# Two-layer streaming encoder on one core: table loads, ScalarE casts and GpSimd blocks are given other places in the queues around the second half's channel norm

## The chip, the cores and the metric

The program runs on one core of one Trainium2 chip. The metric is the device time of one execution in microseconds. The five queues that matter are TensorE (PE, matrix products), VectorE (DVE), ScalarE (ACT), GpSimd (POOL) and SyncE (SP, which issues the transfers). Each engine works through its own instruction queue in order.

## The reference, cut to what matters

Layer 0 mixes an S5 state-space branch and a retention branch; nothing of it is touched. Layer 1 is a Conformer convolution module, and the whole is closed by a root-mean-square norm. The input is 1 x 1024 positions x 1024 channels in float32.

```python
def mixer_conv(h, w_in, conv_w, conv_b, ln_g, ln_b, w_out):
    proj = h @ w_in
    a, b, g = jnp.split(proj, 3, axis=-1)
    u = a * jax.nn.sigmoid(b)
    u = depthwise_conv(u, conv_w, width=31, causal) + conv_b
    mu = jnp.mean(u, axis=-1, keepdims=True)
    var = jnp.mean(jnp.square(u - mu), axis=-1, keepdims=True)
    u = (u - mu) * lax.rsqrt(var + EPS) * ln_g + ln_b
    return (jax.nn.silu(u) * jax.nn.silu(g)) @ w_out

x = x + mixer_conv(rmsnorm(x, norm_g[1]), ...)
return rmsnorm(x, final_g)
```

## The kernel before, in words

Channels lie on the 128 partitions, in eight blocks numbered `nb` or `kb`. Positions lie along a row and are cut in two halves of 512, `h` = 0 and 1. Every product is made of three in a reduced format: a weight block and an operand are each split into a high and a low part (`wh`, `wl`, and for the last product `zh`, `zl`), and `mm3` issues high x high (line 181), high x low (line 182) and low x high (line 183) into one PSUM bank. The high part is a ScalarE copy that rounds (a CAST in the profile), the low part a subtraction on VectorE or GpSimd.

The last product, `w_out_c(h, nb, ...)`, is made of blocks: for each half eight output blocks `nb`, each summing over eight operand blocks `z0` to `z7`, so 24 products of 512 columns. In the text "block (h, nb)" is such an output block. A block takes its weights with `wnext`, which also starts the load of the next two weight blocks in the list: a transfer into `wf`, the ScalarE cast to `wh` (line 171, or line 148 where the low part comes back from DRAM, line 157). `wf`, `wh` and `wl` have three buffers each. When its products are done VectorE adds the residual (line 1649, `x` in the profile), ScalarE squares the sum (line 1650, `s2q`), GpSimd adds the squares up over the blocks (line 1654), and ScalarE multiplies by the final gain (line 1655).

The operand of half 1 becomes ready late. `conv_norm_wide` takes the channel norm of half 1: the last square of the convolution's output (`csquare`, line 1524), two products with a matrix of ones that sum over channels (`wide_sums`, line 487, tile `cst`), then the square of the mean (line 1595), the scaled mean `dl` (line 1598), the variance (line 1599), and in `wide_rsqrt` the factor 1/sqrt as exp(-0.5 ln v) with one Newton step: table load (line 495), Ln (line 497), Exp (line 498), Square (line 499, kept as `self.halved`), two VectorE steps (lines 500 and 501). `conv_scale` then makes the eight operands: scale by the factor (line 1611), subtract (line 1615), SiLU on ScalarE (line 1616), multiply by the gate `gl` (line 1622), split into `zh` and `zl` (lines 1232 and 1234). In half 1 GpSimd does blocks 3, 5 and 7 of these, from a copy `RL` of the factor that ScalarE makes (line 1614), and VectorE does 0, 1, 2, 4 and 6. VectorE's blocks work in a PSUM tile tagged `cv`, of which there are two, so block 2 starts when block 0 has been split, and so on.

A planner orders each engine's queue before the program runs: it simulates the program and takes, for an engine that is free, the ready instruction with the smallest priority number. `self.at(n)` sets that number: the channel norm of half 1 and its operands have 160000, the blocks of half 0 and the first blocks' stage 400000, the blocks (1, 0) to (1, 2) and the final norm of half 0 410000. `issue_after(ins)` adds an edge that holds what is traced under it behind `ins`, but only those instructions that go to the same engine as `ins`; it is an order in that engine's queue and no wait. Blocks (0, 4) to (0, 7) are held for the time in which the norm of half 1 is worked out, so that TensorE has products meanwhile:

```python
blocks(0, range(N0, N0 + 1))
with self.tc.issue_after(self.last_square.ins):
    blocks(0, range(N0 + 1, 8), {N0 + 1: {HOLD: self.norm_mm}, N0 + 2: {0: self.norm_mm}})
```

`N0` is 4, and `last_square` is the ScalarE square of the convolution's block 7. The table of SiLU is named nowhere: the compiler puts a load ahead of the first activation that needs another table (it carries line 1616). After block (1, 2) follow the final norm of half 0 (its sum over channels is tile `rf_R`) and the blocks (1, 3) to (1, 7).

Of the kernel before, what the change touches and what calls it, by code (L numbers as in the profile page):

```python
# [11 lines left out]
F32 = mybir.dt.float32  # L12
F32R = mybir.dt.float32r
I32 = mybir.dt.int32
AF = mybir.ActivationFunctionType
# [37 lines left out]
class Trunk:  # L53
# [432 lines left out]

        self.last_stat = self.nc.tensor.matmul(ps, self.ones[:], a, start=True, stop=True)

    def wide_rsqrt(self, ps, pool, name, scale=1.0):


        nc, v = self.nc, self.nc.vector
        y, half = (pool.tile([P, HALF], F32, name=f"{name}_{tag}", tag=tag, bufs=1) for tag in ("dg", "sq"))
        with self.tc.issue_after(self.squared.ins):
            table = nc.scalar.preload_act_table_set("natural_log_exp_and_others")
        with self.tc.issue_after(table.ins):
            nc.scalar.activation(y[:], ps, AF.Ln, scale=scale, bias=self.epst[:])
        nc.scalar.activation(y[:], y[:], AF.Exp, scale=-0.5)
        self.halved = nc.scalar.activation(half[:], y[:], AF.Square, scale=(0.5 * scale) ** 0.5)
        v.scalar_tensor_tensor(ps, ps, EPS / scale, half[:], op0=ALU.add, op1=ALU.mult)  # L500
        v.scalar_tensor_tensor(ps, ps, 1.5, y[:], op0=ALU.subtract, op1=ALU.mult, reverse0=True)

    def wide_rstd(self, a, pool, name):

# [726 lines left out]
    def split(self, src, hi, lo, eng, behind=None):  # L1231
        self.nc.scalar.copy(hi[:], src)  # L1232
        with self.tc.issue_after(behind.ins) if behind else nullcontext():
            eng.tensor_tensor(lo[:], src, hi[:].bitcast(F32), op=ALU.subtract)

    def layer0_back_and_layer1(self, st):
        nc, A = self.nc, self.A
# [283 lines left out]
        def csquare(h, nb, bank=None):  # L1521
            sq = bank or (self.opA.tile([P, HALF], F32, name=f"cvq{nb}_{h}", tag="A1") if h else
                  lp.tile([P, HALF], F32, name=f"cvq{nb}_{h}", tag="sq", bufs=1))
            self.squared = nc.scalar.activation(sq[:], cv[h][nb][:], AF.Square)
            return sq
# [52 lines left out]
        def conv_norm_wide(sm, acc):  # L1578


            u, w, part, co = self.last_tap
            total = ps_cv.tile([P, HALF], F32, name="cvs_bank", tag="cv")
            v.tensor_tensor(total[:], part[:], sm[:], op=ALU.add)
            v.scalar_tensor_tensor(co[:], u, w, part[:], op0=ALU.mult, op1=ALU.add)
            v.scalar_tensor_tensor(sm[:], u, w, total[:], op0=ALU.mult, op1=ALU.add)
            q7 = csquare(1, 7, ps_cv.tile([P, HALF], F32, name="cvq_bank", tag="cv"))
            self.last_square = self.squared
            self.squares_added = v.tensor_tensor(acc[:], acc[:], q7[:], op=ALU.add)
            s1, s2 = (ps_cv.tile([P, HALF], F32, name=f"cst{i}_1", tag="cn") for i in range(2))
            self.wide_sums(s1[:], sm[:])  # L1590
            self.wide_sums(s2[:], acc[:])
            self.norm_mm = self.last_stat

            m2 = lp.tile([P, HALF], F32, name="cm2_1", tag="dg", bufs=1)
            self.squared = nc.scalar.activation(m2[:], s1[:], AF.Square, scale=1.0 / D)
            dl = lp.tile([P, HALF], F32, name="dl_1", tag="cs", bufs=1)
            with self.tc.issue_after(self.squared.ins):
                nc.scalar.mul(dl[:], s1[:], 1.0 / D)
            v.scalar_tensor_tensor(s2[:], s2[:], 1.0 / D, m2[:], op0=ALU.mult, op1=ALU.subtract)
            self.wide_rsqrt(s2[:], lp, "cn_1")  # L1600
            v.tensor_tensor(dl[:], dl[:], s2[:], op=ALU.mult)
            conv_scale(1, s2, dl)

        def conv_scale(h, Rp, dl):
            R = None
            for nb in range(8):
                c = cv[h][nb]

                e1, e = (v, gp) if h == 0 else (gp, gp) if nb in (3, 5, 7) else (v, v)
                z = ps_cv.tile([P, HALF], F32, name=f"zz{nb}_{h}", tag="cv") if e is v else c  # L1610
                e1.tensor_tensor(z[:], c[:], (R if e1 is gp else Rp)[:], op=ALU.mult)
                if h and nb == 0:
                    R = lp.tile([P, HALF], F32, name=f"RL_{h}", tag="cq", bufs=1)
                    nc.scalar.copy(R[:], Rp[:])
                e.tensor_tensor(z[:], z[:], dl[:], op=ALU.subtract)
                nc.scalar.activation(z[:], z[:], AF.Silu, scale=self.vec(V_LNG, nb), bias=self.vec(V_LNB, nb))
                tag, bufs = ("ld", 2) if h == 0 else ("tp", 3) if nb < 3 else ("u", 5)
                g = lp.tile([P, HALF], F32, name=f"gl{nb}_{h}", tag=tag, bufs=bufs)

                with self.tc.issue_after(self.low_load["ca1"].ins) if h == 0 and nb < 2 else nullcontext():  # L1620
                    nc.sync.dma_start(g[:], self.gs_d[rows(nb), hs(h)])
                e.tensor_tensor(z[:], g[:], z[:], op=ALU.mult)
                pt = (self.opA, "A1") if h and nb == 7 else (opB, f"B{1 - h}")
                a, b = (self.op_tile(*pt, f"z{q}{nb}_{h}") for q in "hl")
                self.split(z[:], a, b, e)
                zs[h][nb] = (a, b)

        final = [[], []]
# [2 lines left out]
        def w_out_c(h, nb, cols, hold=None):  # L1631
# [11 lines left out]
            def part(c):  # L1643
                ps = self.bank(f"mm_oc{nb}_{h}_{c.start}", aux=False)
                n = c.stop - c.start
                self.gemm(ps[:, :n], w, [(a[:, c], b[:, c]) for a, b in zs[h]], hold)
                behind = self.behind.pop(nb, None)
                with self.tc.issue_after(behind.ins) if behind else nullcontext():
                    self.last_add = v.tensor_tensor(t[:, c], ps[:, :n], xt[:, c], op=ALU.add)
                self.squared = nc.scalar.activation(sq[:, c], t[:, c], AF.Square)  # L1650

                if 0 < nb < KB - (h == 1 and c.start > 0):
                    a = final[h][0][1]
                    gp.tensor_tensor(a[:, c], a[:, c], sq[:, c], op=ALU.add)
                nc.scalar.mul(t[:, c], t[:, c], self.vec(V_FG, nb))
            for c in cols:
                yield part(c)

# [48 lines left out]
        for h in range(2):  # L1707
# [20 lines left out]
            with self.at(400000):  # L1728
                if h == 0:
                    blocks(0, range(N0))  # L1730
                    continue

                self.behind = {N0: self.squares_added}
                blocks(0, range(N0, N0 + 1))

                with self.tc.issue_after(self.last_square.ins):
                    blocks(0, range(N0 + 1, 8), {N0 + 1: {HOLD: self.norm_mm}, N0 + 2: {0: self.norm_mm}})
            with self.at(410000):
                blocks(1, range(3))
                with self.tc.issue_after(self.last_mm.ins):  # L1740
# [123 lines left out]
```

## Time and profile before

| what | value |
|---|---|
| time, median of 3 runs (lowest, highest) | 1183.95 us (1183.84, 1184.95) |
| the profiled execution's own time | 1182.88 us |
| its span, first to last instruction | 1181.1 us |
| TensorE busy | 1169.7 us, 99% |
| VectorE, ScalarE, GpSimd busy | 848.4, 490.0, 654.7 us |
| mean granted TensorE clock | 0.999 |

A busy time counts an engine's instructions, not its use; idle time of an engine that does not set the end costs nothing. The timeline of an engine gives start, duration, engine, line, operation, tiles written and read, and in brackets the idle time before the instruction and what ended it. Products overlap, so the distance between two starts is what one product costs.

### The profile page before, as it was taken

To read this page: it belongs to the slowest core of one execution; us is meant where nothing else is said; L and a number is where in the kernel's file an instruction comes from. 1 tells how busy PE (TensorE), PEld (TensorE's weight loads), DVE (VectorE), ACT (ScalarE), POOL (GpSimd) and SP (SyncE) were. 2 spreads that over 40 slices of the span, in tenths; PEclk is the share of its full clock that TensorE was granted. 3 is DMA by queue.
4 is the path that set the end of the run, shared out by engine and by line. 5 is a ranking of instruction groups with operands and counts; after the bars stand their busy time and mean duration, and the time that the engine had idled before them with its cause. 6 is when DMAs were issued, how large, how long until landed. Compare 5 with 4: busy or idle time off the path is not lost.

```text
span 1181.1 us, 17216 instructions
## 1 busy us (share of the span) xinstructions
PE 1169.7 (99%) x6286; PEld 979.1 (83%) x6286; DVE 848.4 (72%) x1464; ACT 490.0 (41%) x719; POOL 654.7 (55%) x448
## 2 busy tenths in 40 slices
PE   9999999999999999999999999999999999999997
PEld 8788888888888888999888888888888888888776
DVE  7975697777418359486679323599999899999744
ACT  6322232322223231333446324445526675444663
POOL 2059999888136354232673111588535567667743
PEclk9999999999999999999999999999999999999999
DMA  9344345655378666769998977656678564367854
GB/s 356 102 135 137 126 150 168 191 179 174 117 266 286 234 220 213 253 221 335 377 340 295 332 261 248 227 183 214 213 251 284 209 191 162 111 200 248 279 189 177
DMA packets 117637, 261.46 MB, mean 221 GB/s; under 512 B 10672, under 2 KB 42288, under 8 KB 116912
## 3 DMA queue, kind: packets, MB, share of 16 engines
q1 hardware_dynamic: 117552, 260.36, 64.9%
q8 instruction: 49, 0.80, 0.3%
q14 instruction: 36, 0.29, 0.1%
HBM read 181.48 MB, written 74.65 MB: 217 GB/s over the span
## 4 chain that ended last, share of the span: by engine, by line
PE 96%; ACT 1%; DVE 1%; DMA 1%; issue 1%; POOL 0%; POOLq 0%; ACTq 0%
PE mm_g L181 8%; PE mm_g L183 7%; PE mm_g L182 7%; PE mm_wo L181 5%; PE mm_wo L182 5%; PE mm_wo L183 5%; PE mm_b L183 2%; PE mm_b L181 2%; PE mm_a L181 2%; PE mm_a L183 2%; PE mm_a L182 2%; PE mm_b L182 2%; PE mm_u L181 2%; PE mm_u L183 2%; PE mm_u L182 2%; PE mm_glu L181 2%
## 5 line engine op out<-in xcount | busy, mean ns | idle before, releaser
L1505 DVE SCALAR_TENSOR_TENSOR cv<-u,convw,cv 128x512 f32<-128x512 f32 x398 | 273.3, 752 | 10.0 <-ACT cv L1484 8.1
L1478 POOL TENSOR_TENSOR tp<-tp,tp 128x512 f32<-128x512 f32 x64 | 83.8, 1309 | 36.7 <-ACT tp L1477 35.6
L181 PE MATMUL mm_g<-xh,wh_g 128*128 128x512 f32 x256 | 101.8, 398 | 0.0
L183 PE MATMUL mm_g<-xh,wl_g 128*128 128x512 f32 x256 | 100.1, 391 | 0.0
L182 PE MATMUL mm_g<-xl,wh_g 128*128 128x512 f32 x256 | 100.0, 391 | 0.0
L415 POOL TENSOR_TENSOR s1q<-s1q,s1q 128x512 f32<-128x512 f32 x12 | 17.7, 1478 | 85.3 <-ACT s1q L410 85.3
L1477 ACT ACTIVATE tp<-u,convw 128x512 f32<-128x512 f32 x64 | 45.3, 719 | 33.6 <-POOL tp L1478 33.5
L181 PEld LDWEIGHTS mm_g<-xh,wh_g 128*128 128x128 f32 x256 | 48.0, 188 | 11.7 <-issue 1.2
L183 PEld LDWEIGHTS mm_g<-xh,wl_g 128*128 128x128 f32 x256 | 48.0, 188 | 10.3
L182 PEld LDWEIGHTS mm_g<-xl,wh_g 128*128 128x128 f32 x256 | 48.1, 188 | 9.9 <-issue 0.4
L371 DVE TENSOR_TENSOR gt<-mm_g,R 128x512 f32<-128x512 f32 x32 | 21.9, 684 | 46.8 <-PE mm_g L183 46.8
L181 PE MATMUL mm_oc<-zh,wh_woc 128*128 128x512 f32 (+1 forms) x144 | 53.0, 375 | 2.3 <-ACT zh L1232 2.3
L182 PE MATMUL mm_oc<-zl,wh_woc 128*128 128x512 f32 (+1 forms) x144 | 52.6, 366 | 0.0
L183 PE MATMUL mm_oc<-zh,wl_woc 128*128 128x512 f32 (+1 forms) x144 | 52.4, 366 | 0.0
L172 POOL TENSOR_TENSOR wl_glu<-wf_glu,wh_glu 128x1024 fp32r<-128x1024 f32 x14 | 34.0, 2428 | 32.9 <-ACT wh_glu L171 20.2
L172 POOL TENSOR_TENSOR wl_v<-wf_v,wh_v 128x1024 fp32r<-128x1024 f32 x12 | 31.2, 2603 | 35.0 <-ACT wh_v L171 35.0
L181 PE MATMUL mm_wo<-ysh,wh_wos 128*128 128x512 f32 x128 | 50.2, 392 | 0.0
L181 PE MATMUL mm_g<-h1h,wh_cg 128*128 128x512 f32 x128 | 50.2, 392 | 0.0
L183 PE MATMUL mm_b<-h1h,wl_cb 128*128 128x512 f32 x128 | 49.9, 390 | 0.0
L182 PE MATMUL mm_b<-h1l,wh_cb 128*128 128x512 f32 x128 | 49.8, 389 | 0.0
L182 PE MATMUL mm_wo<-ysl,wh_wos 128*128 128x512 f32 x128 | 49.8, 389 | 0.0
L183 PE MATMUL mm_g<-h1h,wl_cg 128*128 128x512 f32 x128 | 49.8, 389 | 0.0
(525 smaller groups left out, 3654.6 us busy)
## 6 DMA issues: line engine op xcount, KB each, us to landing
wf_g<-w_ab SPq DMA_DIRECT2D x16, 512.0 KB
wf_wos<-w_out SPq DMA_DIRECT2D x16, 512.0 KB
wf_wor<-w_out SPq DMA_DIRECT2D x16, 512.0 KB
wf_cb<-w_c SPq DMA_DIRECT2D x16, 512.0 KB
wf_ca<-w_c SPq DMA_DIRECT2D x16, 512.0 KB
wf_woc<-w_out_c SPq DMA_DIRECT2D x16, 512.0 KB
wf_v<-w_v SPq DMA_DIRECT2D x12, 512.0 KB
wf_cg<-w_c SPq DMA_DIRECT2D x11, 512.0 KB
```

Of the source, the lines that this page charges most:

```text
L172: self.low_made = lo[i].tensor_tensor(wl[:].rearrange(fl)[:, c], wf[:, c], h.bitcast(F32), op=ALU.subtract)
L181: nc.tensor.matmul(ps, wh[:, kb, :], xh, start=start, stop=False, **more)
L182: nc.tensor.matmul(ps, wh[:, kb, :], xl, start=False, stop=False, **more)
L183: self.last_mm = nc.tensor.matmul(ps, wl[:, kb, :], xh, start=False, stop=stop, **more)
L371: nc.vector.tensor_tensor(gt[:, c], ps[:], self.R[:, c], op=ALU.mult)
L415: nc.gpsimd.tensor_tensor(a, a, sq[:], op=ALU.add)
L1477: nc.scalar.mul(sk[:], u[:, k:k + HALF], cw[:, nb, k:k + 1])
L1478: gp.tensor_tensor(s0[:], s0[:], sk[:], op=ALU.add)
L1505: v.scalar_tensor_tensor(dst[:], *tap, accs_[i][:], op0=ALU.mult, op1=ALU.add)
```

## The change

Five things are done, all around the norm of half 1.

- `log_table`, the load of the table for Ln and Exp, is a function of its own. `conv_norm_wide` calls it first, behind the square of convolution block 6, and the square of block 7 is held behind it. For the other two callers of `wide_rsqrt` nothing changes.
- After `wide_rsqrt` a load of the SiLU table is placed behind `self.halved`, the Square of line 499.
- On ScalarE the squares of blocks (0, 4) to (0, 7) are held behind `halved`, and each final-gain product behind the square of its block. What block (0, 6) issues on ScalarE is held behind `halved`, what block (0, 7) issues there behind the first SiLU of the operands; block (0, 5) stays behind `last_square`.
- On GpSimd the steps of operand block 5 are held behind steps of block 3, and those of block 7 behind steps of block 5, by the table in `behind`.
- GpSimd's sums of squares of blocks (0, 5) to (0, 7) are held behind the low part of operand block 3.

```diff
@@ -486,19 +486,22 @@
 
         self.last_stat = self.nc.tensor.matmul(ps, self.ones[:], a, start=True, stop=True)
 
-    def wide_rsqrt(self, ps, pool, name, scale=1.0):
+    def wide_rsqrt(self, ps, pool, name, scale=1.0, table=None):
 
 
         nc, v = self.nc, self.nc.vector
         y, half = (pool.tile([P, HALF], F32, name=f"{name}_{tag}", tag=tag, bufs=1) for tag in ("dg", "sq"))
-        with self.tc.issue_after(self.squared.ins):
-            table = nc.scalar.preload_act_table_set("natural_log_exp_and_others")
+        table = table or self.log_table()
         with self.tc.issue_after(table.ins):
             nc.scalar.activation(y[:], ps, AF.Ln, scale=scale, bias=self.epst[:])
         nc.scalar.activation(y[:], y[:], AF.Exp, scale=-0.5)
         self.halved = nc.scalar.activation(half[:], y[:], AF.Square, scale=(0.5 * scale) ** 0.5)
         v.scalar_tensor_tensor(ps, ps, EPS / scale, half[:], op0=ALU.add, op1=ALU.mult)
         v.scalar_tensor_tensor(ps, ps, 1.5, y[:], op0=ALU.subtract, op1=ALU.mult, reverse0=True)
+
+    def log_table(self):
+        with self.tc.issue_after(self.squared.ins):
+            return self.nc.scalar.preload_act_table_set("natural_log_exp_and_others")
 
     def wide_rstd(self, a, pool, name):
 
@@ -1231,7 +1234,7 @@
     def split(self, src, hi, lo, eng, behind=None):
         self.nc.scalar.copy(hi[:], src)
         with self.tc.issue_after(behind.ins) if behind else nullcontext():
-            eng.tensor_tensor(lo[:], src, hi[:].bitcast(F32), op=ALU.subtract)
+            return eng.tensor_tensor(lo[:], src, hi[:].bitcast(F32), op=ALU.subtract)
 
     def layer0_back_and_layer1(self, st):
         nc, A = self.nc, self.A
@@ -1578,12 +1581,15 @@
         def conv_norm_wide(sm, acc):
 
 
+
+            table = self.log_table()
             u, w, part, co = self.last_tap
             total = ps_cv.tile([P, HALF], F32, name="cvs_bank", tag="cv")
             v.tensor_tensor(total[:], part[:], sm[:], op=ALU.add)
             v.scalar_tensor_tensor(co[:], u, w, part[:], op0=ALU.mult, op1=ALU.add)
             v.scalar_tensor_tensor(sm[:], u, w, total[:], op0=ALU.mult, op1=ALU.add)
-            q7 = csquare(1, 7, ps_cv.tile([P, HALF], F32, name="cvq_bank", tag="cv"))
+            with self.tc.issue_after(table.ins):
+                q7 = csquare(1, 7, ps_cv.tile([P, HALF], F32, name="cvq_bank", tag="cv"))
             self.last_square = self.squared
             self.squares_added = v.tensor_tensor(acc[:], acc[:], q7[:], op=ALU.add)
             s1, s2 = (ps_cv.tile([P, HALF], F32, name=f"cst{i}_1", tag="cn") for i in range(2))
@@ -1597,32 +1603,47 @@
             with self.tc.issue_after(self.squared.ins):
                 nc.scalar.mul(dl[:], s1[:], 1.0 / D)
             v.scalar_tensor_tensor(s2[:], s2[:], 1.0 / D, m2[:], op0=ALU.mult, op1=ALU.subtract)
-            self.wide_rsqrt(s2[:], lp, "cn_1")
+            self.wide_rsqrt(s2[:], lp, "cn_1", table=table)
+            with self.tc.issue_after(self.halved.ins):
+                nc.scalar.preload_act_table_set("silu_and_others")
             v.tensor_tensor(dl[:], dl[:], s2[:], op=ALU.mult)
             conv_scale(1, s2, dl)
 
         def conv_scale(h, Rp, dl):
-            R = None
+            R, steps = None, {}
+
+            def behind(nb, step, of):
+
+                ins = steps.get((nb - 2, of)) if h and nb in (5, 7) else None
+                return self.tc.issue_after(ins.ins) if ins else nullcontext()
+
             for nb in range(8):
                 c = cv[h][nb]
 
                 e1, e = (v, gp) if h == 0 else (gp, gp) if nb in (3, 5, 7) else (v, v)
                 z = ps_cv.tile([P, HALF], F32, name=f"zz{nb}_{h}", tag="cv") if e is v else c
-                e1.tensor_tensor(z[:], c[:], (R if e1 is gp else Rp)[:], op=ALU.mult)
+                with behind(nb, "scale", "sub" if nb == 5 else "low"):
+                    e1.tensor_tensor(z[:], c[:], (R if e1 is gp else Rp)[:], op=ALU.mult)
                 if h and nb == 0:
                     R = lp.tile([P, HALF], F32, name=f"RL_{h}", tag="cq", bufs=1)
                     nc.scalar.copy(R[:], Rp[:])
-                e.tensor_tensor(z[:], z[:], dl[:], op=ALU.subtract)
-                nc.scalar.activation(z[:], z[:], AF.Silu, scale=self.vec(V_LNG, nb), bias=self.vec(V_LNB, nb))
+                with behind(nb, "sub", "gate"):
+                    steps[nb, "sub"] = e.tensor_tensor(z[:], z[:], dl[:], op=ALU.subtract)
+                silu = nc.scalar.activation(z[:], z[:], AF.Silu, scale=self.vec(V_LNG, nb), bias=self.vec(V_LNB, nb))
+                if nb == 0:
+                    self.first_silu = silu
                 tag, bufs = ("ld", 2) if h == 0 else ("tp", 3) if nb < 3 else ("u", 5)
                 g = lp.tile([P, HALF], F32, name=f"gl{nb}_{h}", tag=tag, bufs=bufs)
 
                 with self.tc.issue_after(self.low_load["ca1"].ins) if h == 0 and nb < 2 else nullcontext():
                     nc.sync.dma_start(g[:], self.gs_d[rows(nb), hs(h)])
-                e.tensor_tensor(z[:], g[:], z[:], op=ALU.mult)
+                with behind(nb, "gate", "low" if nb == 7 else "gate"):
+                    steps[nb, "gate"] = e.tensor_tensor(z[:], g[:], z[:], op=ALU.mult)
                 pt = (self.opA, "A1") if h and nb == 7 else (opB, f"B{1 - h}")
                 a, b = (self.op_tile(*pt, f"z{q}{nb}_{h}") for q in "hl")
-                self.split(z[:], a, b, e)
+                steps[nb, "low"] = self.split(z[:], a, b, e)
+                if nb == 3:
+                    self.third_low = steps[nb, "low"]
                 zs[h][nb] = (a, b)
 
         final = [[], []]
@@ -1647,12 +1668,16 @@
                 behind = self.behind.pop(nb, None)
                 with self.tc.issue_after(behind.ins) if behind else nullcontext():
                     self.last_add = v.tensor_tensor(t[:, c], ps[:, :n], xt[:, c], op=ALU.add)
-                self.squared = nc.scalar.activation(sq[:, c], t[:, c], AF.Square)
+
+                with self.tc.issue_after(self.halved.ins) if h == 0 and nb >= N0 else nullcontext():
+                    self.squared = nc.scalar.activation(sq[:, c], t[:, c], AF.Square)
 
                 if 0 < nb < KB - (h == 1 and c.start > 0):
                     a = final[h][0][1]
-                    gp.tensor_tensor(a[:, c], a[:, c], sq[:, c], op=ALU.add)
-                nc.scalar.mul(t[:, c], t[:, c], self.vec(V_FG, nb))
+                    with self.tc.issue_after(self.third_low.ins) if h == 0 and nb > 4 else nullcontext():
+                        gp.tensor_tensor(a[:, c], a[:, c], sq[:, c], op=ALU.add)
+                with self.tc.issue_after(self.squared.ins):
+                    nc.scalar.mul(t[:, c], t[:, c], self.vec(V_FG, nb))
             for c in cols:
                 yield part(c)
 
@@ -1734,7 +1759,11 @@
                 blocks(0, range(N0, N0 + 1))
 
                 with self.tc.issue_after(self.last_square.ins):
-                    blocks(0, range(N0 + 1, 8), {N0 + 1: {HOLD: self.norm_mm}, N0 + 2: {0: self.norm_mm}})
+                    blocks(0, range(N0 + 1, N0 + 2), {N0 + 1: {HOLD: self.norm_mm}})
+                with self.tc.issue_after(self.halved.ins):
+                    blocks(0, range(N0 + 2, N0 + 3), {N0 + 2: {0: self.norm_mm}})
+                with self.tc.issue_after(self.first_silu.ins):
+                    blocks(0, range(N0 + 3, 8))
             with self.at(410000):
                 blocks(1, range(3))
                 with self.tc.issue_after(self.last_mm.ins):
```

## The prediction

> **What bounds the kernel now.** I read the page first, then TensorE's waits, then the queues of the engines around the longest of them.
>
> ```profile
> span 1181.1 us, 17216 instructions
> PE 1169.7 (99%) x6286; PEld 979.1 (83%) x6286; DVE 848.4 (72%) x1464; ACT 490.0 (41%) x719; POOL 654.7 (55%) x448
> PE 96%; ACT 1%; DVE 1%; DMA 1%; issue 1%; POOL 0%; POOLq 0%; ACTq 0%
> ```
>
> TensorE is busy for 99% of the span and 96% of the chain that ended last is its own. The change removes no product, so it can only win TensorE's holes. Its waits (time in total, times, longest) and its queue around the longest say where they are:
>
> ```profile
> PE mm_oc L181 <- ACT zh L1232: 2.3, 1, 2.3
> PE cst L487 <- DVE cq L1588: 0.4, 1, 0.4
> ```
>
> ```profile
> 1120.91 0.39 PE L183 MATMUL mm_oc<-zh,wl_woc 128*128 128x512 f32 x1
> ...
> 1125.65 0.39 PE L183 MATMUL mm_oc<-zh,wl_woc 128*128 128x512 f32 x1
> 1128.34 0.96 PE L181 MATMUL mm_oc<-zh,wh_woc 128*128 128x512 f32 x3 [2.30 <-ACT zh L1232]
> ...
> 1129.64 0.39 PE L181 MATMUL mm_oc<-zh,wh_woc 128*128 128x512 f32 x1
> ...
> 1140.52 0.40 PE L183 MATMUL mm_oc<-zh,wl_woc 128*128 128x512 f32 x1
> 1140.76 1.02 PE L487 MATMUL rf_R<-s2q,ones 128*128 128x512 f32 x2
> ```
>
> The row at 1120.91 is the last product of block (0, 7); from there to the row `rf_R` TensorE has the 72 products of blocks (1, 0) to (1, 2). The three first products in one row at 1128.34 show that the blocks go side by side, operand by operand. Between 1129.64 (the 24th) and 1140.52 (the 72nd) lie 48 steps without a hole: 10.88 / 48 = 0.2267 us each. Unhindered, the 72 would begin at 1120.91 + 0.23 = 1121.14 and end at 1121.14 + 72 x 0.2267 = 1137.46. `rf_R` starts at 1140.76. So **3.30 us** are lost here: 2.46 in the wait for z2's high part (1128.34 less 1125.65 + 0.23), the rest in small gaps around z0's and z2's arrival. That is the most this change can win at that place. The 0.4 us before `cst` comes before anything that it moves, and stays.
>
> Why z2 is late, on ScalarE, VectorE and GpSimd:
>
> ```profile
> 1096.20 0.63 ACT L1524 ACTIVATE cvq<-co 128x512 f32<-128x512 f32 x1 [2.46 <-DVE co L1505]
> 1098.66 1.05 ACT L171 CAST wh_woc<-wf_woc 128x1024 fp32r<-128x1024 f32 x1 [1.82 <-PE mm_oc L182]
> 1103.01 0.60 ACT L1524 ACTIVATE cvq_bank<-co 128x512 f32<-128x512 f32 x1 [3.30 <-DVE co L1584]
> ...
> 1105.57 0.59 ACT L1598 ACTIVATE dl<-cst 128x512 f32<-128x512 f32 x1
> 1106.17 1.28 ACT L495 ACT_TABLE_LOAD   x1
> 1107.47 0.72 ACT L1655 ACTIVATE x<-x,vecs 128x512 f32<-128x512 f32 x1
> 1108.10 0.61 ACT L1650 ACTIVATE s2q<-x 128x512 f32<-128x512 f32 x1
> 1108.62 0.67 ACT L497 ACTIVATE cn_dg<-cst,epst 128x512 f32<-128x512 f32 x1
> 1109.19 0.71 ACT L1655 ACTIVATE x<-x,vecs 128x512 f32<-128x512 f32 x1
> 1109.81 0.62 ACT L498 ACTIVATE cn_dg<-cn_dg 128x512 f32<-128x512 f32 x1
> 1110.33 1.03 ACT L148 CAST wh_woc<-wf_woc 128x1024 fp32r<-128x1024 f32 x1
> 1111.26 0.63 ACT L499 ACTIVATE cn_sq<-cn_dg 128x512 f32<-128x512 f32 x1
> ...
> 1116.79 1.28 ACT L1616 ACT_TABLE_LOAD   x1
> 1118.08 0.75 ACT L1616 ACTIVATE zz<-zz,vecs 128x512 f32<-128x512 f32 x1
> ...
> 1127.72 0.57 ACT L1232 CAST zh<-zz 128x512 fp32r<-128x512 f32 x1
> ```
>
> ```profile
> 1106.41 0.70 DVE L1599 SCALAR_TENSOR_TENSOR cst<-cst,cm 128x512 f32<-128x512 f32 x1 [0.69 <-PE cst L487]
> 1110.46 0.69 DVE L1649 TENSOR_TENSOR x<-mm_oc,x1l 128x512 f32<-128x512 f32 x1 [3.35 <-PE mm_oc L183]
> 1111.92 0.70 DVE L500 SCALAR_TENSOR_TENSOR cst<-cst,cn_sq 128x512 f32<-128x512 f32 x1 [0.77 <-ACT cn_sq L499]
> ...
> 1114.72 0.70 DVE L1615 TENSOR_TENSOR zz<-zz,dl 128x512 f32<-128x512 f32 x1
> ...
> 1122.38 0.69 DVE L1611 TENSOR_TENSOR zz<-co,cst 128x512 f32<-128x512 f32 x1
> ```
>
> ```profile
> 1115.38 3.80 POOL L1611 TENSOR_TENSOR co<-co,RL 128x512 f32<-128x512 f32 x3 [1.53 <-ACT RL L1614]
> ...
> 1129.14 3.80 POOL L1234 TENSOR_TENSOR zl<-co,zh 128x512 fp32r<-128x512 f32 x3
> ```
>
> Between the scaled mean `dl` and the Square stand a table load, two final-gain products, one square and a weight cast, none of which the factor needs. Before z0's SiLU stands a second load, which nobody asked for early. GpSimd does its three blocks step by step together, so z3 is no sooner than z5 and z7.
>
> **The change part by part.** The sum is made against the profiled execution's own 1182.88 us; the median of the runs shown, 1183.95, is 1.07 above it, and I carry that over.
>
> *Logarithm's table.* It moves to behind the square at 1096.20, which ends at 1096.83; ScalarE is idle then for 1.82 us until 1098.66, so its 1.28 us cost nothing. Were that gap filled, the load would push the cast behind it, and the square of block 7 at 1103.01 is still behind 3.30 us of idleness.
>
> *Factor.* With `dl` done at 1106.16 the Ln now waits for the variance alone: 1106.41 + 0.70 = 1107.11. The final gain of block (0, 3) (0.72) fits in that gap. Then Ln, Exp, Square, 0.67 + 0.62 + 0.63 = 1.92 us back to back: done at 1109.03 and not 1111.89. The gain for VectorE's steps is **2.86 us**, perhaps 0.6 less for z0, because the residual at 1110.46, so far ahead of line 500, now falls among them. TensorE does not see this yet: blocks (0, 5) to (0, 7) cover it until 1121.14.
>
> *SiLU's table.* It runs from 1109.03 to 1110.31, while VectorE makes the factor. z0's subtraction, done at 1115.42 before, is done at 1112.6 to 1113.2, and its SiLU can start then and not at 1118.08: 4.9 to 5.5 us sooner for z0. A load that waits on no data costs 1.28 of ScalarE's time as before, only earlier.
>
> *What was pushed back.* Two squares, two final gains and a cast now stand behind the Square and must run before or among the SiLUs. This is the price, and one row bounds it:
>
> ```profile
> 1106.16:1128.29 22.13, 19.88 (x85) 15.32 (x83) 13.82 (x21) 19.65 (x29) 17.70 (x15) 1.00 0.83 276
> ```
>
> (Columns: length, then busy time of PE, PEld, DVE, ACT, POOL, and the granted clock.) From `dl` to the end of z2's cast ScalarE is busy 19.65 of 22.13 us. Even if the same 29 instructions all stay ahead of that cast, one load leaves: 19.65 - 1.28 = 18.37, so the cast ends at 1106.16 + 18.37 = 1124.5 plus what ScalarE still idles, some 0.5 while it awaits the variance and between dependent steps. That is 1125.0 instead of 1128.29. If SiLUs of later operands and the third cast slip behind it, it is sooner: by VectorE's queue z2's scale at 1122.38 moves up with z0 by 4.9, which would bring the cast to 1123.4. I take 1123.4 to 1125.0.
>
> *When TensorE needs it.* z0 and z1 in three blocks are 18 products: 1121.14 + 18 x 0.2267 = 1125.22. So z2 is just in time. What is late next is the low weights of block (1, 2), whose buffer block (0, 7) frees:
>
> ```profile
>   DMA wl_woc<-lo_woc: 0.3, 1
> ```
>
> That row of TensorE's idle time on these tiles is a wait of 0.3 us for those weights, today ahead of the wait for z2. The transfer's start is set by TensorE's own end of block (0, 7) and does not move, so I keep 0.3, and 0.1 for z2's low half, made 0.7 after the high one. The casts for block (1, 0) and (1, 1), held behind `halved` and the first SiLU, come at about 1111 to 1117; they are needed at 1121 to 1122.
>
> *GpSimd.* It can start its first scale 2.86 us sooner, at 1115.38 - 2.86 = 1112.5. Twelve steps at 3.80 / 3 = 1.27 are 15.2 us, three sums of squares of the same length 3.8, one unhidden SiLU and cast of block 7 about 1.4: z7 is done by 1132.9, against 1129.14 + 3.80 = 1132.94 before. z3 is made first: four steps 5.1, SiLU and cast (0.75 and 0.57 by the rows above) 1.3, done about 1118.9. Side by side TensorE asks for z3 at 1121.14 + 27 x 0.2267 = 1127.3 and for z7 at 1121.14 + 63 x 0.2267 = 1135.4: 2.5 us of margin. The sums of squares are asked for only by `rf_R` at 1137.5.
>
> *After that* everything up to the last product follows TensorE's blocks, whose transfers are started by buffers that TensorE frees, so it moves as a whole; the end behind the last product stays as it is.
>
> Sum: 3.30 won, 0.3 + 0.1 kept: **-2.9 us**. 1182.88 - 2.9 = 1180.0, and with 1.07 a median of 1181.1.
>
> [...] The load at 1106.17 ends at 1107.45 and the next instruction starts at 1107.47, so here 1.28 is the whole price. [...]
>
> **The rivals.** A change below 0.2% of 1183.95, 2.4 us, can't be told from none. In all of them the factor comes sooner.
>
> *Part of the hole stays.* If the pushed-back work costs ScalarE as much as the shorter chain wins, z2 gains only the one load that left its stretch, 1.28: its cast ends at 1127.0, TensorE waits 1.8, and with the small gaps gone about 1.5 is won: 1183.95 - 1.5 = 1182.4. For it speaks 19.65 of 22.13; against it, this grouping of ScalarE's instructions from 1106 to 1129:
>
> ```profile
> L1616 ACT ACTIVATE zz<-zz,vecs 128x512 f32<-128x512 f32 x4 | 2.9, 738 | 0.0
> L1616 ACT ACTIVATE co<-co,vecs 128x512 f32<-128x512 f32 x3 | 2.4, 813 | 0.0
> ```
>
> Seven SiLUs are among the 29, and three of them, of operands 4, 5 and 7, z2 needn't await. The decision lies at 1125.2.
>
> *Slower: the order of the three blocks.* GpSimd's order is now a series, so z7 comes last of all, near 1132.9. If the planner, seeing operands sooner, lets block (1, 0) run to its end before the other two, TensorE reaches z7's low part at 1121.14 + 22 x 0.2267 = 1126.1 and stands until 1132.9; the 50 products left end at 1144.2 against 1140.76: +3.5, or 1187.4. It decides where z7 comes after 1129.4 in that order. Against it: the planner takes what is ready, and by the row at 1128.34 it mixes blocks as soon as an operand lacks.
>
> The granted clock stayed 1.00 over the 2.46 us hole. [...]
>
> *Nothing won.* The compiler still adds its SiLU load, or the 3 us come back as waits for transfers in blocks (1, 3) to (1, 7): 1183.95. Against the first: between the two loads squares and casts ran on either table without a third.
>
> **How the numbers follow.** The forecast, 2.4 to 3.3 won, gets 0.6; the partial gain 0.19, nothing 0.07, slower 0.14. So faster 0.6, same 0.26, slower 0.14. The likeliest case alone is 1180.6 to 1181.6. For 8 in 10 the range takes in noise below (1180.2), the partial case and no gain above (1184.4), and leaves out the slower rival.
>
> **What would show it.** Right: the load of line 495's table near 1097, Square done by 1109.5, no load just ahead of the first SiLU, z2's cast before 1125.5, no wait of `mm_oc` for `zh` above 0.5, `rf_R` near 1137.5 to 1138. Wrong: a wait for `zh` of z2 over 1 us (the first rival), for the low part of z7 (the second), a third load, or a wait of TensorE for `wl_woc`, `wh_woc` or a bank behind 1138.

## The result and the profile after

| | before | after |
|---|---|---|
| median of 10 runs each, taken on one chip (lowest, highest) | 1184.8 us (1183.14, 1185.85) | **1181.3 us** (1180.69, 1182.87) |
| profiled execution: own time, span | 1182.88, 1181.1 us | 1181.03, 1179.2 us |
| first product of the norm (`cst`) to `rf_R`, called *the way* below | 1103.69 to 1140.76: 37.07 us | 1103.35 to 1138.89: 35.54 us |

The ratio is 0.9974, with a 95% interval of 0.9964 to 0.9984: some 3.1 us faster (the two medians differ by 3.5). The prediction said 1181.1. But the two traces differ by only 1.53 us in the way, the one stretch that the change touches. So there are two questions: why the way gained 1.5 and not 2.9, and from where the other 1.5 us of those 3.1 come.

The page of after, its head and the chain that ended last:

```profile
span 1179.2 us, 17214 instructions
PE 1168.7 (99%) x6286; PEld 978.4 (83%) x6286; DVE 850.8 (72%) x1464; ACT 489.0 (41%) x719; POOL 654.2 (55%) x448
PE 96%; POOL 1%; ACT 1%; DVE 1%; issue 1%; DMA 1%; POOLq 0%; SPq 0%; ACTq 0%
```

Same products, and the engines' work is the same within 0.3%. GpSimd has come into the chain with 1%. TensorE's waits in the way, and its queue at the same places as before:

```profile
PE mm_oc L181 <- ACT zh L1235: 0.5, 1, 0.5
PE mm_oc L182 <- POOL zl L1237: 0.4, 1, 0.4
PE cst L487 <- DVE cq L1594: 0.4, 1, 0.4
```

```profile
1103.35 1.13 PE L487 MATMUL cst<-cs,ones 128*128 128x512 f32 x2
...
1120.55 0.39 PE L183 MATMUL mm_oc<-zh,wl_woc 128*128 128x512 f32 x1
...
1135.14 0.39 PE L183 MATMUL mm_oc<-zh,wl_woc 128*128 128x512 f32 x1
1136.01 0.96 PE L181 MATMUL mm_oc<-zh,wh_woc 128*128 128x512 f32 x3 [0.48 <-ACT zh L1235]
...
1137.37 0.50 PE L182 MATMUL mm_oc<-zl,wh_woc 128*128 128x512 f32 x1 [0.40 <-POOL zl L1237]
...
1138.89 1.02 PE L487 MATMUL rf_R<-s2q,ones 128*128 128x512 f32 x2
```

The wait of 2.3 us for z2 is gone. Both new waits belong to operand 7, the last of all. Without them TensorE would have begun it at 1135.14 + 0.23 = 1135.37 and its low part 3 x 0.227 later; it lost 0.64 at the one and 0.68 at the other row, 1.32 us together. From the last product of block (0, 7) to `rf_R` it took 18.34 us, where 73 steps without a hole are 16.55: 1.79 are lost now, 3.30 were before.

ScalarE's queue in after:

```profile
1095.86 0.63 ACT L1527 ACTIVATE cvq<-co 128x512 f32<-128x512 f32 x1 [2.45 <-DVE co L1508]
1096.51 1.28 ACT L504 ACT_TABLE_LOAD   x1
1098.32 1.05 ACT L171 CAST wh_woc<-wf_woc 128x1024 fp32r<-128x1024 f32 x1 [0.53 <-issue]
...
1108.19 0.63 ACT L498 ACTIVATE cn_sq<-cn_dg 128x512 f32<-128x512 f32 x1
1108.84 1.28 ACT L1608 ACT_TABLE_LOAD   x1
...
1113.84 0.73 ACT L1632 ACTIVATE zz<-zz,vecs 128x512 f32<-128x512 f32 x1
...
1120.75 1.05 ACT L148 CAST wh_woc<-wf_woc 128x1024 fp32r<-128x1024 f32 x1 [0.76 <-PE mm_oc L182]
1121.70 0.81 ACT L1632 ACTIVATE co<-co,vecs 128x512 f32<-128x512 f32 x1
1122.42 0.57 ACT L1235 CAST zh<-zz 128x512 fp32r<-128x512 f32 x1
...
1135.34 0.62 ACT L1235 CAST zh<-co 128x512 fp32r<-128x512 f32 x1 [1.40 <-POOL co L1641]
```

The logarithm's load lies in the idle gap and the cast behind it starts as before. The Square is done 5.47 us after `cst` started (8.20 before), z0's SiLU starts after 10.49 (14.39), and z2's cast, the row at 1122.42, ends after 19.64 (24.60). GpSimd's queue in after, from block 5's gate to z7's low part:

```profile
1122.60 1.30 POOL L1641 TENSOR_TENSOR co<-gl,co 128x512 f32<-128x512 f32 x1 [2.24 <-ACT co L1632]
1124.17 1.29 POOL L1237 TENSOR_TENSOR zl<-co,zh 128x512 fp32r<-128x512 f32 x1 [0.28 <-ACT zh L1235]
1125.41 2.68 POOL L1678 TENSOR_TENSOR s2q<-s2q,s2q 128x512 f32<-128x512 f32 x2
1128.04 1.29 POOL L1237 TENSOR_TENSOR zl<-co,zh 128x512 fp32r<-128x512 f32 x1
1129.29 1.29 POOL L1626 TENSOR_TENSOR co<-co,RL 128x512 f32<-128x512 f32 x1
1130.54 1.30 POOL L1678 TENSOR_TENSOR s2q<-s2q,s2q 128x512 f32<-128x512 f32 x1
...
1136.04 1.28 POOL L1237 TENSOR_TENSOR zl<-co,zh 128x512 fp32r<-128x512 f32 x1 [0.73 <-ACT zh L1235]
```

In a series GpSimd stands idle at its hand-overs to ScalarE: 2.24 for block 5's SiLU, which waits on ScalarE behind the weight cast at 1120.75, which itself waits until TensorE frees its buffer. And three sums of squares stand between the steps of the operands. z7 is done at 1136.04 + 1.28 = 1137.32.

### The profile page after: what moved, and what is told of

Read it like the earlier page. It is cut to its first block, busy times and chain, and to the rows that moved or that the text cites. A ratio compares the mean times of both kernels' runs of the same rounds, so it can differ in the third digit from the quotient of the medians.

```text
span 1179.2 us, 17214 instructions
## 1 busy us (share of the span) xinstructions
PE 1168.7 (99%) x6286; PEld 978.4 (83%) x6286; DVE 850.8 (72%) x1464; ACT 489.0 (41%) x719; POOL 654.2 (55%) x448
## 4 chain that ended last, share of the span: by engine, by line
PE 96%; POOL 1%; ACT 1%; DVE 1%; issue 1%; DMA 1%; POOLq 0%; SPq 0%; ACTq 0%
PE mm_g L181 8%; PE mm_g L183 7%; PE mm_g L182 7%; PE mm_wo L182 5%; PE mm_wo L183 5%; PE mm_wo L181 5%; PE mm_b L183 2%; PE mm_b L182 2%; PE mm_a L182 2%; PE mm_b L181 2%; PE mm_a L181 2%; PE mm_a L183 2%; PE mm_u L183 2%; PE mm_u L181 2%; PE mm_u L182 2%; PE mm_glu L181 2%
## 5 line engine op out<-in xcount | busy, mean ns | idle before, releaser
L181 PE MATMUL mm_b<-h1h,wh_cb 128*128 128x512 f32 x128 | 49.8, 389 | 0.0
```

Of the source, the lines that this page charges most:

```text
L181: nc.tensor.matmul(ps, wh[:, kb, :], xh, start=start, stop=False, **more)
```

## The experiments

My theory: the two loads make z2 early, and that is the gain; GpSimd's series takes some of it back at z7. The rival: the casts behind the Square, or the series, are needed for the gain too. And for the 1.5 us that the traces do not show: they come from stretches elsewhere or are noise, or they are no wait at all but TensorE's clock behind the hole. In the table "waits" are TensorE's within the way, in us. Before was run 28, 21 and 34 times beside the kernels of the three groups (e1 to e4; e5 to e8; e9 to e12), with medians of 1184.4, 1183.84 and 1184.08.

| run | the way, us | waits in it, without `cst`'s | median (lowest, highest), us | ratio to before (95%) |
|---|---|---|---|---|
| e1 | 35.08 | low weights 0.4, z3 low 0.3 | 1181.32 (1180.48, 1183.01) | 0.9978 (0.9969, 0.9987) |
| e2 | 35.67 | z3 low 0.9, low weights 0.4 | 1181.8 (1181.04, 1182.73) | 0.9981 (0.9972, 0.9989) |
| e3 | 38.27 | high parts 2.6 in three, z7 low 0.4 | 1184.09 (1183.76, 1185.3) | 1.0 (0.9991, 1.0009) |
| e4 | 34.23 | none | 1180.12 (1179.81, 1182.12) | 0.9969 (0.9958, 0.9981) |
| e5 (before) | 38.65 | z2 high 2.4 | 1184.98, one run | |
| e6 | 34.46 | low weights 0.5 | 1180.23 (1179.62, 1182.4) | 0.9976 (0.9967, 0.9985) |
| e7 | 34.42 | low weights 0.3 | 1180.6 (1179.6, 1181.43) | 0.9971 (0.9962, 0.998) |
| e8 | 34.45 | low weights 0.4 | 1179.93 (1179.58, 1181.3) | 0.9971 (0.9958, 0.9983) |
| e9 | 36.80 | z2 high 0.5 | 1183.41 (1182.18, 1185.26) | 0.9997 (0.9988, 1.0006) |
| e10 | 34.47 | low weights 0.4 | 1180.41 (1179.71, 1183.32) | 0.9976 (0.9968, 0.9985) |
| e11 (after) | 35.58 | z7 high 0.7, low 0.4 | 1181.44 (1180.77, 1183.51) | 0.9981 (0.9972, 0.999) |
| e12 (as e8) | 34.58 | low weights 0.5 | 1180.72 (1179.85, 1183.77) | 0.9974 (0.9965, 0.9982) |

The way repeats within 0.13 us where a kernel was profiled twice (after 35.54 and 35.58, e8 and e12 34.45 and 34.58), while single executions spread over 1.5 to 5 us. So parts are told apart by the way, and the medians are the proof against before. Before alone has two ways, 37.07 and 38.65; that is the clock's question below.

### Which part of the change gains

**e1, the tables alone.** After, without GpSimd's series and without the orders on ScalarE:

```diff
-                ins = steps.get((nb - 2, of)) if h and nb in (5, 7) else None
+                ins = steps.get((nb - 2, of)) if False else None
...
-                    with self.tc.issue_after(self.third_low.ins) if h == 0 and nb > 4 else nullcontext():
+                    with nullcontext():
...
-                    blocks(0, range(N0 + 1, N0 + 2), {N0 + 1: {HOLD: self.norm_mm}})
...
+                    blocks(0, range(N0 + 1, 8), {N0 + 1: {HOLD: self.norm_mm}, N0 + 2: {0: self.norm_mm}})
```

The squares and gains lose their holds too, as in before.

> Only the two table loads are moved; squares, casts and GpSimd's steps are ordered as before. The stage from the last product of block (0, 7) to rf_R took 19.85 us before and 18.34 after, against 16.55 without a hole. Theory (the hole is closed by a shorter ScalarE chain, and the GpSimd series gives part back at z7): the factor comes 1.3 sooner, the SiLU load leaves the front of the first SiLU, GpSimd's blocks stay side by side, so no wait for z7; stage 17.3 to 18.3, time 1.5 to 2.5 below before. Rival (the tables alone are the gain, all the rest is worth nothing): stage 18.3, as after. Rival (GpSimd's order is the gain, z3 sooner): stage 19.3 to 19.9.

The two loads alone give the whole gain: 1181.32 and a way of 35.08, 0.46 shorter than after's. That is 3.1 us below before, more than the 1.5 to 2.5 expected. GpSimd's queue in e1, from its first scale on:

```profile
1114.52 3.80 POOL L1626 TENSOR_TENSOR co<-co,RL 128x512 f32<-128x512 f32 x3
1118.27 3.81 POOL L1631 TENSOR_TENSOR co<-co,dl 128x512 f32<-128x512 f32 x3
1122.03 1.32 POOL L1678 TENSOR_TENSOR s2q<-s2q,s2q 128x512 f32<-128x512 f32 x1
1123.28 3.80 POOL L1641 TENSOR_TENSOR co<-gl,co 128x512 f32<-128x512 f32 x3
1127.02 1.31 POOL L1678 TENSOR_TENSOR s2q<-s2q,s2q 128x512 f32<-128x512 f32 x1
1128.27 3.81 POOL L1237 TENSOR_TENSOR zl<-co,zh 128x512 fp32r<-128x512 f32 x3
```

No idle time at all: while ScalarE works on one block, GpSimd works on the next. z7 is done at 1132.08, 27.8 us after `cst`; in after it is 34.0.

**e2, all but GpSimd's part.** The first two places of e1's diff, that is the series and the hold of the sums, and nothing else.

> The change without its GpSimd part: tables, casts and squares are placed as after, operand blocks 3, 5 and 7 and the sums of squares are left to the planner. Theory: z2 as early as after, no wait of 0.5 and 0.4 us for z7, stage 16.8 to 17.2, time 2.7 to 3.1 below before and 1.2 to 1.5 below after. Rival (GpSimd's order is the gain): z3 is late again, a wait of TensorE for z3 of 1 us or more, stage 18.5 or longer, slower than after.

35.67, 0.6 longer than e1: with the orders on ScalarE z3's low part is waited for 0.9 instead of 0.3. The expectation, a shorter stage and 1.2 to 1.5 us below after, was missed: z7's waits are gone, with z7 done 28.5 us after `cst` instead of 34.0, but z3's came in their place. Set against e2, after's series trades that wait for the two at z7; the way is 0.13 shorter, no more than two profiles of one kernel differ.

**e3, GpSimd's series alone.** Before, with `behind` and the hold of the sums behind `third_low` put in.

> Before with the GpSimd part of the change alone. Theory: z2's wait of 2.3 us stays since ScalarE's chain is as before, z7 is later than before, stage 19.5 to 21, time from no change to 1 us above before. Rival (GpSimd's order is the gain): stage 18.3 or shorter, 1.5 us below before.

With the tables late, the series is a loss of 1.2 us in the way. TensorE's queue in e3 shows four waits instead of one:

```profile
1121.72 0.73 PE L181 MATMUL mm_oc<-zh,wh_woc 128*128 128x512 f32 x2 [0.59 <-ACT zh L1235]
...
1127.58 0.97 PE L181 MATMUL mm_oc<-zh,wh_woc 128*128 128x512 f32 x3 [1.17 <-ACT zh L1235]
...
1138.95 0.97 PE L181 MATMUL mm_oc<-zh,wh_woc 128*128 128x512 f32 x3 [0.84 <-ACT zh L1235]
1140.32 0.50 PE L182 MATMUL mm_oc<-zl,wh_woc 128*128 128x512 f32 x1 [0.39 <-POOL zl L1237]
```

The hole of before is split here: 0.59 for z0, 1.17 for z2, which was expected to keep its 2.3. Yet the median equals before's. So before must lose about 1.2 somewhere that its first trace does not show.

### What holds z7, and a better version

**e4, the three sums on VectorE.** After, with the sums of blocks (0, 5) to (0, 7) taken off GpSimd and held behind operand 6's low part on VectorE:

```diff
-                if nb == 3:
-                    self.third_low = steps[nb, "low"]
+                if nb == 6:
+                    self.sixth_low = steps[nb, "low"]
...
-                    with self.tc.issue_after(self.third_low.ins) if h == 0 and nb > 4 else nullcontext():
-                        gp.tensor_tensor(a[:, c], a[:, c], sq[:, c], op=ALU.add)
+                    late = h == 0 and nb > 4
+                    with self.tc.issue_after(self.sixth_low.ins) if late else nullcontext():
+                        (v if late else gp).tensor_tensor(a[:, c], a[:, c], sq[:, c], op=ALU.add)
```

> The change, with the sums of squares of blocks (0, 5), (0, 6) and (0, 7) taken from GpSimd and given to VectorE behind the low part of operand 6, where VectorE idled 9.88 us. Theory: the three sums of 1.3 us stood in GpSimd's series ahead of z5's low part and z7's steps; without them z7 is done 3.9 us sooner, by about 1133.5, ahead of TensorE's need; the waits of 0.5 and 0.4 go, stage 16.8 to 17.1, time 1.2 to 1.5 us below after. Rival (z7 is late because ScalarE, not GpSimd, hands its SiLU and casts over late): z7 moves by less than 1.5 us, stage 17.8 or longer. Rival (VectorE's sums, two operands in SBUF, hold up GpSimd): GpSimd's steps beside them longer than 1.3 us.

TensorE has no wait left in the way but `cst`'s, and it falls by 1.31 to 34.23, just the 1.32 lost at z7 in after. But z7 itself is only 1.3 us sooner (32.7 after `cst`), not 3 x 1.3 = 3.9, so by z7 alone the first rival's bound of 1.5 is met, and both rivals have a share. GpSimd's and VectorE's queues in e4 say why:

```profile
1128.02 1.29 POOL L1237 TENSOR_TENSOR zl<-co,zh 128x512 fp32r<-128x512 f32 x1 [1.61 <-ACT zh L1235]
1129.27 1.74 POOL L1626 TENSOR_TENSOR co<-co,RL 128x512 f32<-128x512 f32 x1
1131.09 1.62 POOL L1631 TENSOR_TENSOR co<-co,dl 128x512 f32<-128x512 f32 x1
```

```profile
1129.14 4.12 DVE L1679 TENSOR_TENSOR s2q<-s2q,s2q 128x512 f32<-128x512 f32 x3
```

Where sums stood, GpSimd now idles 1.61 for z5's cast; and the two steps that run beside VectorE's sums take 1.74 and 1.62 instead of 1.29.

**e6, e4 without the orders on ScalarE** (the squares' and gains' holds and the split of the blocks taken back as in e1), **e7, e4 without GpSimd's series** (the first place of e1's diff), **e8, e1 with e4's sums**: only the tables and the sums.

> Tables and GpSimd's order as after, the sums of squares on VectorE, but ScalarE's casts, squares and final gains left where the planner puts them. From the first cst product to rf_R it took 35.54 us after, 35.08 with the tables alone, 34.23 with the sums on VectorE. My forecast counted 1.6 us of the factor's 2.86 to the casts and squares: if that reaches TensorE, the way is 34.8 or longer here, with a wait for z2. Rival (TensorE's other products cover the factor, placing casts and squares is worth nothing): 34.2 to 34.5, time within 0.5 us of the kernel with the sums on VectorE.

> Tables and ScalarE placed as after, sums of squares on VectorE, GpSimd's blocks side by side as before. With the sums on GpSimd and no order TensorE waited 0.9 us for z3's low part (way 35.67). Theory (two of the sums stand ahead of z3's low part there, 2.5 us): z3 comes in time, way 34.2 to 34.7, so the series of blocks is worth nothing once the sums are gone. Rival (side by side is itself too slow for z3, four steps of three blocks): a wait for z3 of 0.5 us or more stays, way 35.0 or longer.

> The two table loads moved and the sums of squares on VectorE, nothing else of the change. If the order of GpSimd's blocks and the places of casts and squares are worth nothing beside these two: way 34.2 to 34.7 and the time of the kernel with the sums on VectorE. If ScalarE's places count: 35.0 or longer, with a wait for a high part; if GpSimd's order counts, with a wait for z3's low part.

All three ways lie within 0.04 us of each other, 34.42 to 34.46, and 0.2 above e4's. So once the sums are off GpSimd, neither the orders on ScalarE nor the series is worth more than 0.2 us; what is left of a wait is the 0.3 to 0.5 for the low weights of block (1, 2). In e8 VectorE's sums find GpSimd finished (its last step begins at 1126.64 and lasts 3.79):

```profile
1130.79 2.13 DVE L1679 TENSOR_TENSOR s2q<-s2q,s2q 128x512 f32<-128x512 f32 x3
```

Here three sums take 2.13, beside GpSimd 4.12.

**e10, e8 without the early SiLU load**, which the compiler then places:

```diff
-            with self.tc.issue_after(self.halved.ins):
-                nc.scalar.preload_act_table_set("silu_and_others")
```

> The logarithm's table moved and the sums of squares on VectorE; SiLU's table is left to the compiler, which loads it just ahead of the first SiLU. With both tables the way was 34.45 us. Theory (what counts is what stands ahead of Ln and Square; SiLU's load costs ScalarE 1.28 wherever it stands, and z0's SiLU waited for VectorE anyway): way 34.4 to 34.8, time as with both tables within 0.5 us. Rival (the late load is half of the gain, as the forecast had it: 4.9 us sooner for z0): z2 1.3 later, a wait of TensorE for z2 again, way 35.2 or longer.

The load is back just ahead of the first SiLU (ScalarE in e10):

```profile
1116.72 1.28 ACT L1630 ACT_TABLE_LOAD   x1
1118.01 0.75 ACT L1630 ACTIVATE zz<-zz,vecs 128x512 f32<-128x512 f32 x1
```

z0's SiLU starts 11.31 after `cst` instead of 10.14, but the way is 34.47 against 34.45: z0 has that to spare. So of the five edits the one that is left as the gain is the logarithm's load, in the gap at 1096. No run has it quite alone: in e1 SiLU's load goes with it, in e10 the sums on VectorE do.

**e11 and e12, after and e8 once more**, on one chip with the same runs of before.

> After once more, on one chip with the kernel of the two tables and the sums. Way 35.4 to 35.8 with the waits for z7, time 2.5 to 3.5 us below before.

> The two tables and the sums on VectorE once more beside after: way 34.3 to 34.6, 1.0 to 1.4 us below after and 3.5 to 4.5 below before, if the stage is all that differs. Rival (both are the same within the spread of the executions): less than 0.5 us below after.

The two tables with the sums on VectorE are 1.0 us shorter in the way and 0.72 lower in the median than the change, where 1.0 to 1.4 had been expected. That beats before clearly; against after it is shown by the traces, while the intervals of the two ratios overlap.

### Where the other 1.5 us come from

**e5, before once more**, unchanged, to have a second trace of it.

> Before once more, to see how much one profiled execution differs from another. The sums of the stages in the profiles give 1.5 us between before and after, the medians 3.1. If before's profiled execution was a short one, this one's time is nearer 1184.4 than 1182.9 and the extra lies outside the stage; if the stage itself varies, the way from the first cst product to rf_R differs from 37.07 us by 0.5 or more.

The same wait, 2.44 instead of 2.30, but the way is 1.58 us longer. TensorE's queue and the windows from 1128 on in e5 (columns: length, busy time of PE, PEld, DVE, ACT, POOL, granted clock, DMA share, GB/s):

```profile
1128.84 1.65 PE L181 MATMUL mm_oc<-zh,wh_woc 128*128 128x512 f32 x3 [2.44 <-ACT zh L1232]
1130.28 0.63 PE L182 MATMUL mm_oc<-zl,wh_woc 128*128 128x512 f32 x1
1130.71 0.63 PE L183 MATMUL mm_oc<-zh,wl_woc 128*128 128x512 f32 x1
```

```profile
1128.00:1130.00 2.00, 1.16 (x3) 0.97 (x4) 1.46 (x3) 2.00 (x5) 2.00 (x3) 0.72 0.49 187
1130.00:1132.00 2.00, 2.00 (x7) 1.52 (x6) 1.44 (x3) 1.36 (x3) 2.00 (x2) 0.50 0.00 0
1132.00:1134.00 2.00, 2.00 (x10) 1.65 (x9) 1.02 (x2) 0.81 (x2) 1.42 (x2) 0.93 0.04 8
```

The same window of the first trace of before, and of after:

```profile
1130.00:1132.00 2.00, 2.00 (x11) 1.65 (x10) 1.18 (x3) 1.09 (x2) 2.00 (x3) 1.00 0.04 8
```

```profile
1130.00:1132.00 2.00, 2.00 (x11) 1.65 (x10) 0.00 (x0) 0.00 (x0) 2.00 (x3) 1.00 0.00 0
```

Behind the hole the products follow each other at 0.43 instead of 0.227 us, at a granted clock of 0.50. The three windows lack 2 x (0.28 + 0.50 + 0.07) = 1.7 us of full clock, so it was at half for some 3.4 us. Such a stretch lowers the mean clock of an execution by 1.7 / 1183 = 0.0014, and that mean is recorded for every run. The 83 runs of before beside the experiments, by mean clock:

| mean granted clock | runs of before | median | runs of the other kernels (121 in all, after among them) |
|---|---|---|---|
| 0.997 | 29 | 1184.53 us | none |
| 0.998 | 21 | 1184.58 us | 57 |
| 0.999 | 33 | 1182.97 us | 64 |

Before has two times, 1.6 us apart, as its two ways are (1.58). The first trace (clock 0.999, own time 1182.88) is of the one kind, e5 (0.997, 1184.98) of the other. By their times the 50 runs at 0.997 and 0.998 are of the longer kind; this is inferred from clock and time, for only e5's fall stands in a trace. In the other kernels 0.998 and 0.999 go with no such step: the medians at the two differ by -0.9 to +0.9 us, either way round. In the traces of before and after the clock is at 0.50 once more at the very end, behind TensorE's last product, for 3.4 and 3.9 us of the span. That alone gives means of 1 - 3.4 / (2 x 1181.1) = 0.9986 and 1 - 3.9 / (2 x 1179.2) = 0.9983, recorded as 0.999 and 0.998, so its length moves the mean between the two. So without the fall of the clock before takes 1182.97; after's 1181.3 to 1181.44 is 1.5 to 1.7 below that, the 1.53 of the traces. e3's 1184.09 is 1.1 above it, its 1.2 in the way. Both sums close.

**e9, the hole filled.** Before, with eight small products, whose result nobody reads, put where TensorE waits for z2:

```diff
+                if i == 1:
+                    self.second = self.last_mm
...
+                with self.at(405000), self.tc.issue_after(self.second.ins):
+                    fill = self.bank("fill")
+                    for _ in range(8):
+                        nc.tensor.matmul(fill[:, :P], self.ones[:], self.ones[:], start=True, stop=True)
```

> Before, with eight products of ones, read by nobody, put into TensorE's hole behind the second operand of block (1, 2). Before's two profiled executions took 37.07 and 38.65 us from the first cst product to rf_R; in the second the granted clock was 0.50 for 3.4 us behind the hole of 2.4 us, in the first it stayed 1.00. Theory (in many executions the hole itself lowers the clock, and that is why the medians differ by more than the stages): the way is 36.9 to 37.3 with the clock at 1.00, and the time is 0.8 to 1.5 us below before, though z2 is as late as ever. Rival (the executions differ elsewhere, the clock is rare): the same time as before, within 0.5 us.

The wait falls to 0.5 and none of the 11 runs has a clock of 0.997, where 29 of 83 had it before. But the median is only 0.7 below that of before beside it, less than the expected 0.8 to 1.5, and the ratio's interval holds 1: by time alone this run is inconclusive. It stands 0.4 above the 1182.97 of before without the fall; what costs that was not settled. (Executions also differ ahead of the way: in the profiled one of e9, 1185.26 us long, `cst` starts at 1106.33, in before's at 1103.69.)

## Why the prediction came out

The number was right, 1181.1 against 1181.3, and so was the mechanism in the main; its sum was not. **Two terms were wrong, and they cancel**, so that the number came out so near is luck. Of its own signs, the load near 1097 (1096.51), the Square by 1109.5 (1108.82) and z2's cast before 1125.5 (1122.99) came; `rf_R` near 1137.5 to 1138 did not (1138.89), and the wait for z7's low part, its sign for the second rival, did come, with 0.4.

*The factor.* Right: the load fits the gap, and the Square is 2.73 sooner against `cst` (forecast 2.86).

*SiLU's table.* z0's SiLU came 3.9 sooner, not 4.9 to 5.5, since two final gains, two squares, a cast and the copy of the factor now stand ahead of it on ScalarE. That the early load pays was not borne out (e10 against e8, both with the sums on VectorE: 0.02 in the way). In e10, too, the load takes 1.28 and the next instruction starts 0.01 later (1118.01, by the rows above).

*The pushed-back work.* Right: z2's cast came 4.96 sooner (forecast 3.3 to 4.9), and no wait for z2 is left. The first rival, that this work eats the gain, fell. The low weights' wait, kept at 0.3, was read from the weight load; between TensorE's products it cost 0.08 in before (1124.54 to 1124.85, a step being 0.23), no wait of a product for it stands in after, and it is 0.3 to 0.5 where z7 is early.

*GpSimd: the mis-sized term.* The forecast had z7 done at 1132.9 with 2.5 us of margin, "one unhidden SiLU and cast", 1.4. It was done at 1137.32. Of the 4.42 us, 0.89 are the later start (1113.39 for 1112.5, behind the copy of the factor), 0.24 the steps, and 3.3 the hand-overs to ScalarE: GpSimd idles 4.7 us in its series, at five places, not at one. e2 and e7 show that it is the series: e2, which leaves out GpSimd's part alone, has no idle time there and z7 done 28.5 us after `cst` (after: 34.0), and e7, which is e4 without the series, has 26.2 (e4: 32.7). z3 too came later than forecast, at 1125.46 and not at 1118.9, since its cast at 1123.42 stood behind that weight cast on ScalarE; no product waited for it. The sum of 2.9 lost 1.32 to it and came to 1.53.

*The second rival's place was right*, z7 in a series; its mechanism was not, for the blocks did mix, and its price of 3.5 was too high.

*The 1.07 us carried over.* The forecast took the distance between the profiled execution and the median as noise that stays. It is the half clock behind the hole, by the table in 50 of 83 runs, and goes with the hole. The sentence "the granted clock stayed 1.00 over the 2.46 us hole" was true of that one execution. With 1182.88 - 1.53 = 1181.35 and nothing carried over, the median is met.

## What to carry to other kernels

A table load, 1.28 us here, cost nothing in a gap of 1.82 us (after) nor ahead of an operand with time to spare (e10, 0.02 in the way); between the steps of the chain it stood in the way (the Square is done 8.20 us after `cst` in before, 5.98 in e10). So move the one in front of the chain first, and look whether the other's user has time to spare. Blocks done in a series on GpSimd left it idle at the hand-overs to ScalarE (4.7 us in after); side by side they hid it (no idle time in e1), so take foreign work off that engine before its order is changed. Compare the mean clock of all runs of a kernel before one profile is taken for typical: here a hole of 2.4 us cost TensorE its length and, in more than half of the executions, 1.6 us more.

## What the runs showed of the hardware

**The clock behind a short hole.** After 2.44 us without a product (e5) the clock was at 0.50 for some 3.4 us, by the three windows above; after 2.30 us in another execution of the same program it stayed at 1.00. Holes of up to 1.17 us (e3) left it at 1.00. Around the hole e5 (first) and the first trace of before (second) look like this, in the same columns as above:

```profile
1126.00:1128.00 2.00, 0.40 (x2) 0.00 (x0) 1.06 (x2) 2.00 (x4) 2.00 (x2) 1.00 0.93 316
1128.00:1130.00 2.00, 1.16 (x3) 0.97 (x4) 1.46 (x3) 2.00 (x5) 2.00 (x3) 0.72 0.49 187
```

```profile
1126.00:1128.00 2.00, 0.04 (x1) 0.00 (x0) 1.36 (x2) 2.00 (x4) 2.00 (x3) 1.00 0.86 297
1128.00:1130.00 2.00, 1.66 (x7) 1.29 (x8) 1.64 (x3) 2.00 (x5) 2.00 (x2) 1.00 0.33 125
```

TensorE has 1.56 us of products in these 4 us of e5 and 1.70 in the first trace, and the two holes differ by 0.14 us. What decides between the two was not shown. How often the clock fell is inferred from the table of mean clocks: in 50 of 83 runs of before, 60%.

**VectorE and GpSimd beside each other.** Three sums on VectorE took 4.12 us beside two GpSimd steps (e4) and 2.13 without (e8), the steps 1.74 and 1.62 (e4) instead of 1.29 (after). One after the other the five would take 2.13 + 2 x 1.29 = 4.71 us; beside each other they took 4.12, 0.59 less. So both engines were slower beside each other, and together still faster than in turn. Why was not shown.
